# Seven sums over the partitions: two fp32r products of a split operand in place of one fp32 product

## The chip, the cores and the metric

The kernel runs on one core of a Trainium2 chip. The metric is device time in microseconds (us) of one execution, start to end. Before the change it is 1109.1 us, the median of three runs (1109.07 to 1109.46).

Five engines work side by side, each through its own list of instructions in order: TensorE (PE, matmuls), VectorE (DVE), ScalarE (ACT), GpSimd (POOL) and SyncE (SP), which here only issues DMAs. An instruction that has to wait holds up all that stands behind it on its engine. `fp32r` is a 4-byte type that the kernel feeds to PE's fast matmuls; a plain `float32` (fp32) operand makes PE take a slower kind of matmul.

## The reference

One layer of an encoder block over 272 positions (16 learned meta tokens and 256 tokens) of width 2048, all in float32:

```python
hn = rmsnorm(h, mix_norm_g)                # x * rsqrt(mean(x*x) + eps) * g
q_a, k_a, v_a, cq, ckv, k_pe = split(hn @ w_in)
# group A: 8 heads of 2-D neighbourhood attention; q_a and k_a get an rmsnorm per head
# group B: 8 heads of latent attention:
#   q = rmsnorm(rmsnorm(cq) @ w_q_up),  kv = rmsnorm(ckv) @ w_kv_up
#   k = rmsnorm([k_nope, k_pe]),  then a rotation of the last 64 dimensions of q and k
mix = concat(rmsnorm(out_a), rmsnorm(out_b))
h = h + mix @ w_out
h = h + (silu(conv3(rmsnorm(h) @ w_gate)) * (rmsnorm(h) @ w_up)) @ w_down
```

Every rmsnorm needs a sum of squares over the features.

## The kernel before

**Layout and tiling.** Activations stand transposed: features over the 128 partitions, positions along the row (272 columns, or 258 where only the tokens and two meta tokens next to them are needed). A sum over features is therefore a sum over the partitions. The kernel first adds the squares of all 128-row tiles element by element, and then multiplies the one tile that is left with a 128x128 matrix of ones on PE: each output row is the sum over the partitions. That matmul is `ones_sum(sq, n)` (line 763). Both operands of it are fp32.

**Splits.** All large products are made exact enough by splitting: a value is the sum of a high part `hi`, rounded to fp32r, and a low part `lo`, the rest. ACT writes the high part, DVE the low part (`split_plain`, line 976; for the weights `split_hi` and `split_lo`, lines 549 and 567, which write the tiles `whi` and `wlo`). A product is three fp32r matmuls: hi*hi, hi*lo, lo*hi (`mm3`, line 603, recorded as L606, L607, L608). PE's other matmuls are recorded as L278 (`MM`) and its transposes as L284 (`TR`).

**The seven sums.** `ones_sum` is called for: x (`scale_x`, line 795, 272 columns), the query latent (`scale_cq`, 838, 258), the key/value latent (`compressed_kv`, 850, 272), the rotary key (`rotary_key`, 901, 272), the output of each attention group (`group_scale`, 1484, called twice, 258) and h ahead of the MLP (`scale_h`, 1528, 258). The sum of x's squares is added up in the tile `sqx` by POOL, 15 additions in `sum_x` (line 739), each as soon as ACT has squared a tile. When the last is done, the event `ev_sum_x` is set, and `scale_x` goes on: it copies `ones` on DVE into the fp32r tile `ones_r` (for other sums, in `keys` and `small_sums`, that use two fp32r products already), then asks for `ones_sum(sqx, L)`, and makes the norm's factor from its result.

**The norms' weights.** `make_gains` (line 926) multiplies columns of the weight table `vecs` into a tile `gains`: three DVE operations on 128x1, issued when `vecs` has landed. `gains` is used by the keys and queries of the attention heads, from 66 us on.

**What sets the order.** The kernel is written as Python generators, one thread per piece of work. Each `yield` asks for an engine with a cost in ns, or for an event, or for a buffer. A planner (`Flow`, line 99 on) runs them in simulated time when the program is built, and the order in which it serves them is the order of the instructions on each engine. A request can start at the thread's time plus a latency: 700 ns towards PE (`TO_PE`), 200 away from PE, 140 between the others; of several that could start at the same moment, the one with the smaller priority number goes first. The costs are formulas: a `tensor_tensor` of DVE counts 68 + 1.04 ns for each column, so a weight split of 512 columns 600; an fp32 product of 272 columns 460, an fp32r one 124. What the chip does later changes nothing in the order. Buffers come from pools (`Slots`), such as `sps`, two PSUM banks for sums and scores, and `scr`, nine scratch tiles.

Of the kernel before, what the change touches and what calls it, by code (L numbers as in the profile page):

```python
# [10 lines left out]
F32R = mybir.dt.float32r  # L11
# [4 lines left out]
P = 128  # L16
# [4 lines left out]
L = SEQ + N_META  # L21
# [184 lines left out]
def encoder_block(ctx: ExitStack, tc: tile.TileContext, io):  # L206
    nc = tc.nc
    ctx.enter_context(tc.manual_schedule())
    fl = Flow()
# [6 lines left out]
    apool = actx.enter_context(tc.tile_pool(name="apool", bufs=1))  # L216

    def tiles(pool, n, shape, name, dt=F32):
        return [pool.tile(shape, dt, tag=f"{name}{i}", name=f"{name}{i}") for i in range(n)]


    def size(ap):
        n = 1
        for s in ap.shape[1:]:
            n *= s
        return n
# [4 lines left out]
    def columns(*scalars):  # L231
        return sum(not (s is None or isinstance(s, float)) for s in scalars)

    def ACT(out, in_, f, **kw):
        ns = (51 if in_psum(in_) else 93) + 0.833 * size(in_)
        ns += 93 * (columns(kw.get("scale")) + columns(kw.get("bias")) > 0)
        yield "act", ns + 113 * ("accum_out" in kw)
        nc.scalar.activation(out, in_, f, **kw)  # L238

    def TT(out, a, b, op):  # L240
        yield "dve", 68 + 1.04 * size(out)
        nc.vector.tensor_tensor(out, a, b, op)  # L242

    def TS(out, a, s0, s1, *ops):
        yield "dve", 68 + 62 * columns(s0, s1) + (1.04 if in_psum(a) else 0.52) * size(out)
        nc.vector.tensor_scalar(out, a, s0, s1, *ops)  # L246

    def STT(out, a, s, b, op0, op1):
        yield "dve", 68 + 62 * columns(s) + 1.04 * size(out)
        nc.vector.scalar_tensor_tensor(out, a, s, b, op0, op1)  # L250

    def COPY(out, a):
        yield "dve", 68 + 1.04 * size(out)
        nc.vector.tensor_copy(out, a)
# [13 lines left out]
    def cost(l, r):  # L268
        n, m = size(r), l.shape[-1]
        if r.dtype != F32R:  # L270
            return max(1.69 * n, 3.33 * m, 50)
        return 0.445 * n + 3 if n >= 256 else max(0.84 * n, 0.84 * m, 27)

    def MM(items):

        yield "pe", sum(cost(l, r) for _, l, r, _, _ in items)
        for o, l, r, start, stop in items:
            nc.tensor.matmul(o, l, r, start=start, stop=stop)  # L278
# [18 lines left out]
    def one(slots):  # L297
        (t,) = yield slots, 1
        return t
# [172 lines left out]
    n = len(others) - BEHIND  # L472
# [145 lines left out]
    def vec(name, i=0):  # L618
        c = VECS[name] + i
        return vecs[:, c : c + 1]  # L620

    def const(name, n=P):
        return consts[:, CONSTS[name] : CONSTS[name] + n]

    ones = const("ones")
# [126 lines left out]
    ev_sum_x = Event()  # L752


    def rstd(out, v, a):

        yield from ACT(out, v, AF.Ln)
        yield from ACT(out, out, AF.Exp, scale=-0.5)
        yield from ACT(a, out, AF.Square)
        yield from STT(a, v, -0.5, a, ALU.mult, ALU.mult)  # L760
        yield from STT(out, a, 1.5, out, ALU.add, ALU.mult)

    def ones_sum(sq, n):
        s = yield from one(sps)
        yield from MM([(s[:, :n], ones, sq, True, True)])
        return s

    def token_columns(row, small, main):


        yield "pool", 150
        nc.gpsimd.tensor_copy(few_t, repeated(row[:, SEQ:NT], 2))
        pt = yield from one(tps)
        yield from TR(
            [(pt[:4, :P], few_t.rearrange("p c t -> p (c t)")), (pt[:, P : 2 * P], row[:, :P]),
             (pt[:, 2 * P : 3 * P], row[:, P:SEQ])]
        )
        yield from COPY(small, pt[:4, 0:1])
        for c in range(2):
            for i in range(2):  # L780
                j = 2 * c + i
                yield from COPY(main[:, j : j + 1], pt[:, (i + 1) * P : (i + 1) * P + 1])
        fl.put(tps, pt)

    s1 = apool.tile([P, L], F32, name="s1")
    ones_r = apool.tile([P, P], F32R, name="ones_r")
# [5 lines left out]
    ev_em1, ev_s1, ev_em1c, ev_emc, ev_ones = Event(), Event(), Event(), Event(), Event()  # L792
    ev_kr, ev_ekpe = Event(), Event()

    def scale_x():
        yield ev_sum_x
        yield ev_consts
        yield from COPY(ones_r, ones)
        fl.set(ev_ones)
        m1, a = yield scr, 2  # L800
        ss = yield from ones_sum(sqx, L)
        yield from TS(m1[:, :L], ss[:, :L], 1.0 / D_MODEL, EPS, ALU.mult, ALU.add)
        fl.put(sps, ss)
        yield from TS(em1, m1[:, :L], EPS, None, ALU.mult)
        fl.set(ev_em1)
        yield from rstd(s1, m1[:, :L], a[:, :L])
        fl.put(scr, m1)
        fl.put(scr, a)
        fl.set(ev_s1)
        yield from token_columns(em1[:, :NT], em1_s, em1_c)  # L810
        fl.set(ev_em1c)
# [26 lines left out]
    def scale_cq():  # L838
        yield ev_cqs
        yield ev_em1  # L840
        t = sum_cq[:, :NT]
        ss = yield from ones_sum(t, NT)
        yield from STT(t, ss[:, :NT], 1.0 / Q_RANK, em1[:, :NT], ALU.mult, ALU.add)
        fl.put(sps, ss)
        yield from TS(t, t, EPS, None, ALU.mult)
        yield from token_columns(t, emc_s, emc_c)
        fl.put(scr, sum_cq)
        fl.set(ev_emc)

    def compressed_kv(pss):  # L850
        t0, t1, a, b, r = yield scr, 5
        ts = (t0, t1)
        for i, ps in enumerate(pss):
            yield from ACT((a, b)[i][:, :L], ps[:, :L], AF.Square)
        fl.spawn(latent_gained(pss, ts))
        yield from TT(a[:, :L], a[:, :L], b[:, :L], ALU.add)
        yield ev_em1
        ss = yield from ones_sum(a[:, :L], L)
        v = b[:, :L]
        yield from STT(v, ss[:, :L], 1.0 / KV_RANK, em1, ALU.mult, ALU.add)  # L860
        fl.put(sps, ss)
        yield from rstd(r[:, :L], v, a[:, :L])
        for i, t in enumerate(ts):
            fl.spawn(latent_scaled(i, t, r))
        for i in range(2):
            yield ev_ckvs[i]
        for t in (a, b, r):
            fl.put(scr, t)
        fl.set(ev_ckv)
# [55 lines left out]

    def make_gains():
        yield ev_vecs
        yield from STT(gains[:, 0:1], vec("g_naq"), HD ** -0.5, vec("g_nak"), ALU.mult, ALU.mult)
        yield from STT(gains[:, 1:2], vec("g_qn"), QK_DIM ** -0.5, vec("g_kn"), ALU.mult, ALU.mult)
        yield from TS(gains[:, 2:3], vec("g_qp"), QK_DIM ** -0.5, None, ALU.mult)  # L930
        fl.set(ev_gains)
# [44 lines left out]
    def split_plain(hi, lo, src):  # L976
        yield from ACT(hi, src, AF.Copy)
        yield from TT(lo, src, hi.bitcast(F32), ALU.subtract)
# [1048 lines left out]

    fl.spawn(first_loads())
    fl.spawn(make_gains())

    fl.spawn(split_x(), 2)
    fl.spawn(split_hi(), lambda: -1 if 16 < n_split[0] < at[0] + 2 else 2)
    fl.spawn(split_lo(), lambda: -1 if 16 < n_split[1] < at[0] + 2 else 2)
    fl.spawn(square_x(), lambda: 3 if sq_n[0] < 10 else 0)
    fl.spawn(sum_x(), 3)
    fl.spawn(scale_x())
    fl.spawn(scale_cq())
    fl.spawn(attention_weights(), 1)
# [159 lines left out]
```

## Time and profile before

| | |
|---|---|
| median of three runs | 1109.1 us |
| the profiled execution | 1109.03 us, of which the span from first to last instruction is 1107.2 us |
| PE busy | 1101.4 us (99%) |
| DVE busy | 990.3 us (89%) |
| ACT busy | 733.8 us (66%) |
| POOL busy | 140.7 us (13%) |
| granted TensorE clock | 1.0 |
| starts of the seven sums' products on PE | 36.3, 39.4, 45.4, 63.2, 280.0, 296.6 and 388.5 us |
| POOL's additions into `sqx` | 15, from 15.0 us on, the last begins at 34.7 us |
| `gains` on DVE | three operations, 23.2 to 25.7 us |

In the timeline, a row has the start, the time that the instruction (or a run of equal ones) took, the engine, the line, the operation, the output and input tiles, shapes, and how many there are; in brackets stands idle time of the engine before it, and what ended that. Matmuls overlap: a new one can start before the one ahead has ended, so their price is the distance between starts. An fp32 product shows as two matmul rows.

### The profile page before, as it was taken

The numbers are of one execution on the slowest core, as the hardware profiler recorded it, in microseconds if no ns is written. First come the engines' busy times: TensorE is split into PE (matmuls) and PEld (weight loads), VectorE is DVE, ScalarE is ACT, GpSimd is POOL, SyncE is SP. The second block draws the span as 40 slices with busy tenths as digits, with TensorE's granted clock in tenths as the row PEclk, the third lists the DMA queues.
The fourth block names the chain that finished last, engine by engine and source line by source line (L and its number), as shares of the span: only waits on it lengthen the run. The fifth ranks groups of instructions, "written<-read, shape, count | busy, mean of one in ns | idle before, by whom it ended". The sixth has DMA issues, their size and how long they took to land.

```text
span 1107.2 us, 22547 instructions
## 1 busy us (share of the span) xinstructions
PE 1101.4 (99%) x8414; PEld 1062.7 (96%) x8414; DVE 990.3 (89%) x1834; ACT 733.8 (66%) x1467; POOL 140.7 (13%) x202
## 2 busy tenths in 40 slices
PE   9999999999999999999999999999999999999998
PEld 9999999999999999999999999999999988888888
DVE  8879888888868989999999999988988999999984
ACT  8688979898647766656666565655556565655663
POOL 3311222121333400000000000000000011100114
PEclk9999999999999999999999999999999999999999
DMA  9553434444655696657656577777678787777862
GB/s 326 196 171 124 150 125 151 139 162 134 230 188 159 208 342 226 194 189 241 222 196 230 178 244 242 235 236 244 202 277 297 263 297 250 252 258 262 284 250 77
DMA packets 72374, 239.41 MB, mean 216 GB/s; under 512 B 8136, under 2 KB 12744, under 8 KB 72264
## 3 DMA queue, kind: packets, MB, share of 16 engines
q1 hardware_dynamic: 71976, 237.69, 63.7%
q8 instruction: 66, 1.08, 0.4%
q14 instruction: 44, 0.36, 0.1%
q10 hardware_dynamic: 288, 0.27, 0.1%
HBM read 219.44 MB, written 17.83 MB: 214 GB/s over the span
## 4 chain that ended last, share of the span: by engine, by line
PE 93%; ACT 3%; DVE 3%; issue 1%; POOL 0%; DVEq 0%; POOLq 0%; ACTq 0%
PE bank L278 24%; PE bank L606 19%; PE bank L607 19%; PE bank L608 19%; PE bank L1857 6%; PE bank L1858 3%; PE bank L284 2%; ACT whi L238 1%; DVE scr L250 1%; ACT scr L238 1%; DVE wlo L242 0%; PE bank L698 0%; DVE cols L258 0%; ACT mqr L238 0%; DVE p L246 0%
## 5 line engine op out<-in xcount | busy, mean ns | idle before, releaser
L238 ACT ACTIVATE whi<-raw 128x512 fp32r<-128x512 f32 (+2 forms) x479 | 357.8, 764 | 171.8 <-PE bank L607 91.0
L242 DVE TENSOR_TENSOR wlo<-raw,whi 128x512 fp32r<-128x512 f32 (+2 forms) x479 | 415.1, 885 | 46.8 <-ACT whi L238 44.7
L606 PE MATMUL bank<-hl,whi 128*128 128x258 f32 (+2 forms) x1528 | 438.9, 287 | 0.1
L607 PE MATMUL bank<-hl,whi 128*128 128x258 f32 (+2 forms) x1528 | 433.7, 284 | 0.0
L608 PE MATMUL bank<-hl,wlo 128*128 128x258 f32 (+2 forms) x1528 | 432.9, 283 | 0.0
L608 PEld LDWEIGHTS bank<-hl,wlo 128*128 128x128 f32 x1528 | 290.1, 190 | 0.6 <-DVE wlo L242 0.6
L607 PEld LDWEIGHTS bank<-hl,whi 128*128 128x128 f32 x1528 | 289.6, 190 | 0.1
L606 PEld LDWEIGHTS bank<-hl,whi 128*128 128x128 f32 x1528 | 288.5, 189 | 0.5 <-ACT scr L238 0.4
L238 ACT ACTIVATE whi<-quarters 128x1024 fp32r<-128x1024 f32 x88 | 81.5, 950 | 64.7 <-PE bank L1857 44.4
L278 PE MATMUL bank<-whi,act 128*128 128x256 f32 (+1 forms) x420 | 111.5, 317 | 0.0
L1857 PE MATMUL bank<-act,whi 128*128 128x512 f32 x308 | 109.9, 397 | 0.0
L242 DVE TENSOR_TENSOR wlo<-quarters,whi 128x1024 fp32r<-128x1024 f32 x88 | 99.5, 1156 | 10.6 <-ACT whi L238 10.1
L266 POOL TENSOR_TENSOR mt<-mt,mt 128x256 f32<-128x256 f32 x7 | 6.9, 986 | 652.3 <-ACT mt L238 652.3
L1858 PE MATMUL bank<-act,wlo 128*128 128x256 f32 x308 | 86.4, 280 | 0.0
L278 PE MATMUL bank<-whi,sin 128*128 128x512 f32 (+1 forms) x272 | 83.5, 355 | 0.0
L278 PEld LDWEIGHTS bank<-whi,act 128*128 128x128 f32 x420 | 74.1, 189 | 5.7
L1857 PEld LDWEIGHTS bank<-act,whi 128*128 128x128 f32 x308 | 57.8, 188 | 13.8
L278 PE MATMUL bank<-whi,hl 128*128 128x256 f32 x288 | 66.5, 280 | 0.0
L278 PE MATMUL bank<-wlo,act 128*128 128x256 f32 (+1 forms) x210 | 66.3, 315 | 0.0
L238 ACT ACTIVATE whi<-more_raw 128x1024 fp32r<-128x1024 f32 (+2 forms) x46 | 44.1, 962 | 23.9 <-PE bank L607 11.6
L1858 PEld LDWEIGHTS bank<-act,wlo 128*128 128x128 f32 x308 | 58.1, 189 | 1.6
L278 PEld LDWEIGHTS bank<-whi,sin 128*128 128x128 f32 x272 | 49.5, 188 | 7.7
(276 smaller groups left out, 1948.8 us busy)
## 6 DMA issues: line engine op xcount, KB each, us to landing
raw<-in_w_gate SPq DMA_DIRECT2D x83, 512.0 KB, 5.0
raw<-in_w_in SPq DMA_DIRECT2D x52, 512.0 KB, 4.1
raw<-in_w_up_s SPq DMA_DIRECT2D x44, 512.0 KB, 4.8
quarters<-in_w_down_s SPq DMA_DIRECT2D x44, 512.0 KB, 6.9
raw<-in_w_up SPq DMA_DIRECT2D x34, 512.0 KB, 5.4
raw<-in_w_out SPq DMA_DIRECT2D x32, 512.0 KB, 3.9
raw<-in_w_down SPq DMA_DIRECT2D x32, 512.0 KB, 5.0
s_down<-sums SPq DMA_DIRECT2D x22, 512.0 KB, 4.0
```

Of the source, the lines that this page charges most:

```text
L238: nc.scalar.activation(out, in_, f, **kw)
L242: nc.vector.tensor_tensor(out, a, b, op)
L250: nc.vector.scalar_tensor_tensor(out, a, s, b, op0, op1)
L266: nc.gpsimd.tensor_tensor(out, a, b, op)
L278: nc.tensor.matmul(o, l, r, start=start, stop=stop)
L284: nc.tensor.transpose(o, i, ident[:n, :n])
L606: nc.tensor.matmul(ps, whi, xhi, start=start, stop=False)
L607: nc.tensor.matmul(ps, whi, xlo, start=False, stop=False)
L608: nc.tensor.matmul(ps, wlo, xhi, start=False, stop=stop)
L1857: nc.tensor.matmul(ps, whi, x, start=start, stop=False)
L1858: nc.tensor.matmul(ps[:, :n], wlo, x[:, 0, :], start=False, stop=stop)
```

## The change

`ones_sum` now splits its operand first: a new pair of fp32r tiles (`parts_sq`, one pair for all seven calls) takes the high part from ACT and the low part from DVE, and PE multiplies each with `ones_r`, adding both in one PSUM bank. Because `ones_r` has to be there, `ones_sum` waits for the event that its copy sets, and `scale_x` makes that copy before it waits for the sum of x's squares, not after. `make_gains` waits for the sum of x's squares too.

```diff
+    parts_sq = Slots(tiles(apool, 1, [P, 2, L], "parts_sq", F32R))
+
     def ones_sum(sq, n):
+
+        parts = yield from one(parts_sq)
+        hi, lo = (parts[:, i, :n] for i in range(2))
+        yield from split_plain(hi, lo, sq)
+        yield ev_ones
         s = yield from one(sps)
-        yield from MM([(s[:, :n], ones, sq, True, True)])
+        yield from MM([(s[:, :n], ones_r, hi, True, False), (s[:, :n], ones_r, lo, False, True)])
+        fl.put(parts_sq, parts)
         return s
...
     def scale_x():
-        yield ev_sum_x
         yield ev_consts
         yield from COPY(ones_r, ones)
         fl.set(ev_ones)
+        yield ev_sum_x
         m1, a = yield scr, 2
         ss = yield from ones_sum(sqx, L)
...
     def make_gains():
         yield ev_vecs
+        yield ev_sum_x
         yield from STT(gains[:, 0:1], vec("g_naq"), HD ** -0.5, vec("g_nak"), ALU.mult, ALU.mult)
```

## The prediction

> **What bounds the kernel now.** The page comes first: busy times, the chain that ended last, and what an engine waited for.
>
> ```profile
> PE 1101.4 (99%) x8414; PEld 1062.7 (96%) x8414; DVE 990.3 (89%) x1834; ACT 733.8 (66%) x1467; POOL 140.7 (13%) x202
> ...
> PE 93%; ACT 3%; DVE 3%; issue 1%; POOL 0%; DVEq 0%; POOLq 0%; ACTq 0%
> ```
>
> TensorE is the bound from end to end: 93% of the chain is PE. So an edit is worth what it takes from PE's stream of matmuls, or what it makes that stream wait. The seven sums lie in three places; the view of stages shows how full the others are there.
>
> ```profile
> 22.00:36.00 14.00, 13.97 (x111) 13.61 (x110) 13.86 (x23) 13.72 (x34) 10.38 (x10) 1.00 0.67 216
> 36.00:50.00 14.00, 14.00 (x111) 13.64 (x110) 11.44 (x34) 7.88 (x19) 0.88 (x2) 1.00 0.68 228
> 50.00:100.00 50.00, 49.48 (x398) 48.13 (x397) 41.55 (x105) 40.85 (x122) 7.16 (x16) 1.00 0.46 143
> ...
> 200.00:300.00 100.00, 100.00 (x829) 99.06 (x828) 87.36 (x222) 81.64 (x244) 24.59 (x42) 1.00 0.50 164
> ...
> 383.00:430.00 47.00, 47.00 (x394) 46.94 (x393) 40.57 (x83) 32.24 (x58) 2.55 (x2) 1.00 0.80 286
> ```
>
> Columns: stretch, length, then busy time of PE, its weight loads, DVE, ACT, POOL. From 22 to 36 us, right before the first sum, DVE is busy 13.86 of 14.00 us. In the other stretches shown it has an eighth or more to spare. The clock is 1.00 throughout, so it plays no part.
>
> **Part 1: the product itself.** PE's timeline around the first sum (fp32, 272 columns), the fifth (fp32, 258) and a sum that is two fp32r products already:
>
> ```profile
> 36.14 0.29 PE L608 MATMUL bank<-hl,wlo 128*128 128x272 f32 x1
> 36.27 0.62 PE L278 MATMUL bank<-sqx,consts 128*128 128x272 f32 x2
> 36.52 0.49 PE L606 MATMUL bank<-hl,whi 128*128 128x272 f32 x1
> 36.85 0.29 PE L607 MATMUL bank<-hl,whi 128*128 128x272 f32 x1
> ...
> 76.79 0.41 PE L278 MATMUL bank<-late,ones_r 128*128 128x272 f32 x2
> 77.04 0.29 PE L606 MATMUL bank<-hl,whi 128*128 128x272 f32 x1
> ...
> 280.04 0.60 PE L278 MATMUL bank<-sum_b,consts 128*128 128x258 f32 x2
> 280.28 0.47 PE L606 MATMUL bank<-ob,whi 128*128 128x258 f32 x1
> 280.59 0.29 PE L607 MATMUL bank<-ob,whi 128*128 128x258 f32 x1
> 280.71 0.28 PE L608 MATMUL bank<-ob,wlo 128*128 128x258 f32 x1
> ```
>
> Matmuls overlap, so their price is the distance of starts. The first sum and the matmul behind it take 36.85 - 36.27 = 0.58 us; such a matmul alone takes 0.13 (36.14 to 36.27), so the fp32 product costs 0.45. The matmul behind it is where half of that sits: it starts 0.33 before its successor, not 0.13. The two fp32r products cost 77.04 - 76.79 = 0.25, with no mark left on the next matmul. Gain: 0.20. With 258 columns it is (280.59 - 280.04) - 0.12 = 0.43 against 2 x 0.12 = 0.24, gain 0.19. Three sums have 272 columns (x, the kv latent, the rotary key), four have 258 (the q latent, two groups, h): 3 x 0.20 + 4 x 0.19 = **-1.36 us**, and all of it lies on PE. The Trainium skill ("FP8 and Floating Point Precision", TensorE Precision Notes) counts true fp32 as four passes; here it is two recorded matmuls of together 0.45 us, not four of 0.125, so by the page the seven would give 7 x 0.25 = 1.75 and the total below would be 0.4 lower; I go by the rows.
>
> **Part 2: the norms' weights (`make_gains`) move.** Three tiny DVE operations run at 23 to 26 us, and PE shows this:
>
> ```profile
> 22.91 1.02 POOL L746 TENSOR_TENSOR sqx<-sqx,pt 128x272 f32<-128x272 f32 x1 [0.58 <-DMA raw<-in_w_in]
> 23.21 0.73 DVE L250 SCALAR_TENSOR_TENSOR gains<-vecs 128x1 f32<-128x1 f32 x1
> 23.87 0.68 DVE L242 TENSOR_TENSOR wlo<-raw,whi 128x512 fp32r<-128x512 f32 x1
> 24.37 0.29 PE L607 MATMUL bank<-hl,whi 128*128 128x258 f32 x1
> 24.47 0.73 DVE L250 SCALAR_TENSOR_TENSOR gains<-vecs 128x1 f32<-128x1 f32 x1
> 24.60 0.39 PE L608 MATMUL bank<-hl,wlo 128*128 128x258 f32 x1
> 24.82 0.29 PE L606 MATMUL bank<-hl,whi 128*128 128x258 f32 x1
> 25.12 0.49 DVE L250 SCALAR_TENSOR_TENSOR hl<-pt,hl 128x272 fp32r<-128x272 f32 x1
> 25.53 0.14 DVE L246 TENSOR_SCALAR gains<-vecs 128x1 f32<-128x1 f32 x1
> 25.60 0.68 DVE L242 TENSOR_TENSOR wlo<-raw,whi 128x512 fp32r<-128x512 f32 x1
> 26.02 0.28 PE L607 MATMUL bank<-hl,whi 128*128 128x258 f32 x1
> 26.33 0.39 PE L608 MATMUL bank<-hl,wlo 128*128 128x258 f32 x1
> 26.55 0.28 PE L606 MATMUL bank<-hl,whi 128*128 128x258 f32 x1
> ```
>
> They hold DVE for (23.87 - 23.21) + (25.12 - 24.47) + (25.60 - 25.53) = 1.38 us, each ahead of a low part (`wlo`) that PE needs next. PE loses (24.82 - 24.37) - 0.24 = 0.21 and (26.55 - 26.02) - 0.24 = 0.29. With the three gone the low parts come 0.66 and 1.38 earlier, more than the waits. **-0.50 us**, kept if nothing else is late next (part 3).
>
> Behind the sum each would cost between 0.07 (the last one's distance) and 0.73; I take 0.25 for the three, by the last one, since POOL has nothing to do then (it ends its adds at 35.56, see below). The Trainium skill ("SBUF", Who interferes with whom) says that a DVE operation with two SBUF inputs and a GpSimd one that reads SBUF exclude each other; the row agrees (0.73 us for 128x1 beside the add from 22.91 on). If 0.73 held wherever they stand, the wait of part 3 would grow by 1.2 us.
>
> **Part 3: the split ahead of the product.** Each sum now needs ACT (high part), then DVE (low part), then PE. Alone these are small: an ACT pass over 128x272 from this trace is 0.43 us, a DVE one 0.43 (rows below). What counts is the order. The planner sets each engine's order by its own costs. It puts a product at least 700 ns behind the planned end of what feeds it (`TO_PE`), and counts a DVE split of 128x512 as 600. Before, the first sum's thread copies `ones_r` on DVE and only then asks for its product. The chip shows:
>
> ```profile
> 27.09 8.47 POOL L746 TENSOR_TENSOR sqx<-sqx,pt 128x272 f32<-128x272 f32 x7 [1.91 <-ACT pt L238]
> ...
> 28.78 1.18 ACT L238 ACTIVATE late<-bank,vecs 128x258 fp32r<-128x258 f32 x3
> 29.62 1.79 DVE L250 SCALAR_TENSOR_TENSOR late<-bank,vecs,late 128x258 fp32r<-128x258 f32 x4
> ...
> 34.84 2.47 DVE L242 TENSOR_TENSOR wlo<-raw,whi 128x512 fp32r<-128x512 f32 x3
> 37.24 0.21 DVE L254 CAST ones_r<-consts 128x128 fp32r<-128x128 f32 x1
> 37.38 0.68 DVE L242 TENSOR_TENSOR whi<-raw,whi 128x512 fp32r<-128x512 f32 x1
> 37.98 0.68 DVE L242 TENSOR_TENSOR wlo<-raw,wlo 128x512 fp32r<-128x512 f32 x1
> ...
> 44.29 0.43 DVE L242 TENSOR_TENSOR scr<-scr,scr 128x272 f32<-128x272 f32 x1
> 45.65 0.15 DVE L254 COPY emc_s<-bank 4x1 f32<-4x1 f32 x1 [0.93 <-PE bank L284]
> ...
> 39.64 0.43 ACT L238 ACTIVATE s<-scr 128x272 f32<-128x272 f32 x1 [3.74 <-DVE scr L246]
> ```
>
> The copy ran at 37.24 to 37.45, but the product planned 0.7 behind it had started at 36.27. So DVE is 37.45 + 0.70 - 36.27 = 1.9 us late against PE here: beside POOL's adds of x's squares three splits take 37.24 - 34.84 = 2.40, not 1.8, and the work before them is stretched likewise. Today nobody feels it, because the product reads `sqx`, ready at 35.56. After the change the product reads a DVE result, and PE, in order, stands before it. The wait is 1.9 - 0.7 = 1.2, less the rounding up to the next free place between groups of three matmuls (0 to 0.37, mean 0.2), plus the 0.50 that PE has gained in part 2. DVE does not keep its own gain of 1.38: its four operations from 29.62 on take their input from ACT's (28.78 on), whose order and length are unchanged. That is 1.5. Counted forward it is the same: 37.24 for DVE, the three moved operations 0.25, one split 0.60, the low part 0.43, so 38.5; PE's place is three groups later, 36.27 + 9 x 0.126 - 0.50 = 36.9; wait 1.6. I take **+1.5 us**, bounds 0 (the planner finds the low part a place ahead of splits that are not ready) and 2.7 (the 0.73 of part 2).
>
> On ACT the high part stands before the adds' end at 35.56 and holds the weight splits behind it for about a microsecond; ACT then idles 3.74 us before 39.64 anyway, which covers it. Without that cover it would be another 1.3 (0.9 of waiting, 0.4 of work).
>
> At the other six sums I take 0. At the q latent and the kv latent PE is itself 1.5 later than planned, so DVE is late by 0.4 against it, under the 0.7; by 45.65 DVE even idles 0.93. The rotary key, the groups and h have DVE an eighth free, and the results have time: the groups' sums are needed after the first output products, h's after a whole pair of gate tiles. Cover gone, each costs up to 0.43 + 0.43. The early copy of `ones_r` waits for `consts`, long landed where the planner puts it: 0.
>
> **Sum**, against the profiled execution's 1109.03 (span 1107.2 and 1.8 around it; the median is 1109.1): -1.36 - 0.50 + 1.50 = -0.36, so 1108.7.
>
> **Rivals.**
> - *No wait at the first sum.* Only gains are left: -1.86, 1107.2. For it: the planner might put the product later. Against: DVE's 1.9 us are measured, and the lead it leaves is 0.7.
> - *The planner's new order clears old waits.* Everything behind 22 us is sorted anew. From 50 to 100 us PE issues 398 matmuls; at the rate of 200 to 300 us (829 in 100) it would be 414, so some 16 x 0.12 = 2 us may be waits there. All gone: 1108.7 - 2.0 = 1106.7. Against: nothing in the change aims at them, and an order can lose as much.
> - *Slower: DVE's lateness is not used up by the first wait.* If the gains, three low parts and the splits that ACT held back keep DVE over 0.7 us late at the q and kv latents too, PE waits 1.5 at each of three sums: -1.86 + 4.5 = +2.6, 1111.7. It decides from a DVE lateness of 0.7 on at 39 us. For it: DVE is nearly full until 44.7. Against: the idle 0.93 before 45.65.
> - *The product's saving isn't PE's.* If the gap behind an fp32 product were there anyway, part 1 gives half: 1109.4. The row at 77.04 speaks against.
>
> **How the numbers follow.** Forecast 0.48, no wait 0.20, new order 0.15, slower 0.12, half the saving 0.05. What a measurement can tell from no change is about 0.2%, 2.2 us: under 1106.9 or over 1111.3. Faster: the new order, and a third of "no wait" with luck in the order, 0.22. Slower 0.12; the rest 0.66. The range runs from 1106.8 to 1110.7: below it lies half of the new order, above it the slower case; its upper part holds the 2.7 bound (1109.9) and some loss by order.
>
> **What would show it.** Two fp32r matmuls per sum, 0.25 apart from the next, seven times. No gap in PE at 24.6 and 26.3. One new gap of 1.2 to 1.7 us in PE before the first sum's product, put down to DVE's low part, with that part at about 38. Wrong if PE has no such gap, if it has gaps at the second and third sum, or if waits between 50 and 300 us move the end by more than this sum.

## The result, and the profile after

The changed kernel takes 1112.07 us (median, 1111.67 to 1113.54); the kernel before, in the same session, 1109.18 (1108.95 to 1109.84). The ratio is 1.0026, 95% interval 1.0017 to 1.0036: slower by 2.9 us, where 0.4 less was forecast. The profiled execution took 1112.18 us.

The page of the changed kernel: span, busy times, and the chain that ended last.

```profile
span 1110.1 us, 22546 instructions
PE 1100.5 (99%) x8414; PEld 1062.4 (96%) x8414; DVE 994.0 (90%) x1841; ACT 737.0 (66%) x1474; POOL 143.4 (13%) x202
PE 93%; ACT 2%; DVE 2%; issue 1%; DMA 1%; POOL 0%; SPq 0%; DVEq 0%; POOLq 0%; ACTq 0%
```

PE is the bound as before, with 0.9 us less to do (1101.4 before); DVE and ACT have seven instructions more each, the splits. The span is 2.9 us longer all the same, so PE must stand idle longer. Where, the view of stages tells. Of the kernel before, the stretch from 48 to 131 us (columns as in the prediction: stretch, length, busy PE, weight loads, DVE, ACT, POOL, clock, DMA share, GB/s):

```profile
48.00:131.00 83.00, 82.31 (x675) 80.78 (x674) 70.75 (x182) 71.28 (x220) 14.57 (x33) 1.00 0.46 147
```

Of the changed kernel, the stages of the prediction and that stretch:

```profile
22.00:36.00 14.00, 13.87 (x111) 13.54 (x110) 13.86 (x22) 11.85 (x31) 8.89 (x10) 1.00 0.66 223
36.00:50.00 14.00, 12.91 (x104) 12.56 (x103) 11.96 (x36) 9.46 (x22) 1.44 (x2) 1.00 0.69 222
...
200.00:300.00 100.00, 100.00 (x831) 99.03 (x831) 87.41 (x229) 82.42 (x249) 23.99 (x43) 1.00 0.48 162
383.00:430.00 47.00, 47.00 (x395) 46.97 (x394) 41.66 (x82) 34.12 (x61) 4.46 (x4) 1.00 0.83 295
...
48.00:131.00 83.00, 79.96 (x658) 78.44 (x657) 70.39 (x182) 70.48 (x217) 18.60 (x33) 1.00 0.44 149
```

In the two stages shown behind 200 us nothing is lost. From 36 to 50 us PE is busy 12.91 of 14.00 instead of 14.00: the wait at the first sum, which the prediction has. From 48 to 131 us it is busy 79.96 instead of 82.31, so 2.35 us are lost where the prediction had none. The waits of PE, of the kernel before (for what, on what; us in total, times, longest):

```profile
PE bank L698 <- DVE em L695: 1.1, 1, 1.1
PE bank L278 <- POOL sq8r L266: 0.5, 2, 0.3
```

and of the changed kernel:

```profile
PE bank L278 <- POOL sq8r L266: 2.0, 2, 1.7
PE bank L278 <- DVE gains L246: 1.1, 1, 1.1
PE bank L698 <- DVE em L695: 1.1, 1, 1.1
PE bank L606 <- ACT qraw L238: 0.7, 2, 0.4
PE bank L278 <- DVE mkp L242: 0.5, 1, 0.5
PE bank L284 <- POOL p L266: 0.2, 1, 0.2
```

The second line is the first sum (the profile names the DVE operation right behind the low part). The others that are new or longer (`sq8r`, `qraw`, `mkp`, `p`) have no part in the seven sums: they belong to the heads' queries, keys and scores.

**PE's lag** puts it in order. Take the start of the n-th matmul of PE's commonest kind (L606, the first of each triple; 1860 in both kernels) and subtract that of the kernel before. Worked out from the two traces:

| from, to (us, time of before) | lag grows by | what lies there | forecast |
|---|---|---|---|
| to 19.8 | +0.30 | start, landing of the first DMAs | |
| 19.8 to 32.1 | -0.34 | the norms' weights are gone from here | -0.50 |
| 32.1 to 37.1 | +0.39 - 0.45 | a new wait at 35.2; the first product has not run yet (it had before) | 0 |
| 37.1 to 38.6 | +1.72 | first sum: two products and their wait; with the -0.45 above +1.27 | -0.20 + 1.50 |
| 38.6 to 60 | -0.41 | q and kv latent | -0.39 |
| 60 to 64.4 | -0.20 | rotary key | -0.20 |
| 64.4 to 131.4 | **+2.21** | heads of both groups | 0 |
| 131.4 to 266.8 | +0.01 | | 0 |
| 266.8 to 310 | -0.33 | the two groups' sums | -0.38 |
| 310 to 416 | -0.15 | h's sum | -0.19 |
| 416 to the end | +0.21 | | 0 |

Together +2.96. One line of this table is out of the forecast by more than 0.5 us, and it is 2.21. The first line differs from execution to execution (-0.28 to +1.25 at 19.8 us in the traces of the kernels below). Where work is in another order, a lag inside such a stretch can be off by a few tenths of a microsecond and more; the marks from 38.6 us on stand where the lag over all 8414 matmuls is the same.

The places that the prediction named, in the changed kernel's PE timeline:

```profile
24.59 0.29 PE L607 MATMUL bank<-hl,whi 128*128 128x258 f32 x1
24.75 0.39 PE L608 MATMUL bank<-hl,wlo 128*128 128x258 f32 x1
24.97 0.28 PE L606 MATMUL bank<-hl,whi 128*128 128x258 f32 x1
...
35.22 0.29 PE L607 MATMUL bank<-hl,whi 128*128 128x272 f32 x1
35.63 0.39 PE L608 MATMUL bank<-hl,wlo 128*128 128x272 f32 x1
35.86 0.29 PE L606 MATMUL bank<-hl,whi 128*128 128x272 f32 x1
...
37.39 0.39 PE L278 MATMUL bank<-parts_sq,ones_r 128*128 128x272 f32 x1
38.87 0.39 PE L278 MATMUL bank<-parts_sq,ones_r 128*128 128x272 f32 x1 [1.08 <-DVE gains L246]
39.10 0.29 PE L606 MATMUL bank<-hl,whi 128*128 128x272 f32 x1
...
286.51 0.41 PE L278 MATMUL bank<-parts_sq,ones_r 128*128 128x258 f32 x2
286.75 0.49 PE L284 MATMUL bank<-ident,p 128*128 128x128 f32 x3
```

The high part's product starts at 37.39; the low part's could follow 0.13 later, at 37.52, and starts at 38.87: a wait of 1.35. The fifth sum takes 286.75 - 286.51 = 0.24. The gap at 24.6 has shrunk to (24.97 - 24.59) - 0.24 = 0.14, the one at 26.3 to 0.09, and there is one of (35.86 - 35.22) - 0.25 = 0.39 at 35.2.

DVE of the changed kernel in front of the first sum:

```profile
26.57 4.61 DVE L242 TENSOR_TENSOR wlo<-raw,whi 128x512 fp32r<-128x512 f32 x5
...
37.64 0.15 DVE L250 SCALAR_TENSOR_TENSOR gains<-vecs 128x1 f32<-128x1 f32 x1
37.71 0.68 DVE L242 TENSOR_TENSOR whi<-raw,whi 128x512 fp32r<-128x512 f32 x1
38.31 0.15 DVE L250 SCALAR_TENSOR_TENSOR gains<-vecs 128x1 f32<-128x1 f32 x1
38.38 0.43 DVE L242 TENSOR_TENSOR parts_sq<-sqx,parts_sq 128x272 fp32r<-128x272 f32 x1
```

The low part ends at 38.81 (forecast 38.5). The norms' weights cost 0.15 each now, not 0.73, as taken.

### The profile page after: what moved, and what is told of

It is laid out like the page before. It is cut to its first block, busy times and chain, and to the rows that moved or that the text cites. A ratio compares the mean times of both kernels' runs of the same rounds, so it can differ in the third digit from the quotient of the medians.

```text
span 1110.1 us, 22546 instructions
## 1 busy us (share of the span) xinstructions
PE 1100.5 (99%) x8414; PEld 1062.4 (96%) x8414; DVE 994.0 (90%) x1841; ACT 737.0 (66%) x1474; POOL 143.4 (13%) x202
## 4 chain that ended last, share of the span: by engine, by line
PE 93%; ACT 2%; DVE 2%; issue 1%; DMA 1%; POOL 0%; SPq 0%; DVEq 0%; POOLq 0%; ACTq 0%
PE bank L278 25%; PE bank L606 19%; PE bank L607 19%; PE bank L608 19%; PE bank L1866 6%; PE bank L1867 3%; PE bank L284 2%; ACT whi L238 1%; DVE wlo L242 1%; ACT scr L238 1%; DMA scr<-scr 0%; DMA raw<-in_w_in 0%; DVE scr L250 0%; PE bank L698 0%; POOL sq8r L266 0%
## 5 line engine op out<-in xcount | busy, mean ns | idle before, releaser
L606 PE MATMUL bank<-hl,whi 128*128 128x258 f32 (+2 forms) x1528 | 437.8, 287 | 0.0
L606 PEld LDWEIGHTS bank<-hl,whi 128*128 128x128 f32 x1528 | 288.7, 189 | 0.1
L238 ACT ACTIVATE whi<-more_raw 128x1024 fp32r<-128x1024 f32 (+2 forms) x46 | 44.1, 962 | 24.6 <-PE bank L607 9.8
```

What stands on the lines that cost most here:

```text
L606: nc.tensor.matmul(ps, whi, xhi, start=start, stop=False)
```

## The experiments

Theory at the start: the splits are more work on DVE and ACT, and the waits from 62 us on are theirs. Its rival: the planner, told of other costs, issues the same work in another order from 48 us on (in the traces, PE's order is another up to about 200 us), and it is that order which PE waits in. Growth of the lag is that from 60 to 131 us, and from there to 266 us. It holds the rotary key's product, so 0.2 less where that one is two fp32r products; 131 us lies inside the stretch of another order in some kernels, so the sum of the two columns is surer than each.

| kernel | us | ratio (95%) | 60 to 131 | 131 to 266 |
|---|---|---|---|---|
| the change | 1112.07 | 1.0026 (1.0017 to 1.0036) | +2.01 | +0.01 |
| `gains_only` | 1108.95 | 1.0000 (0.9991 to 1.0008) | +0.01 | -0.07 |
| `sums_only` | 1111.82 | 1.0025 (1.0016 to 1.0034) | +1.91 | +0.07 |
| `x_fp32` | 1111.59 | 1.0021 (1.0012 to 1.0030) | +1.91 | 0.00 |
| `late3` | 1108.78 | 0.9996 (0.9987 to 1.0005) | -0.03 | +0.01 |
| `late3_gains` | 1109.12 | 0.9997 (0.9989 to 1.0006) | -0.03 | +0.09 |
| `after_order_fp32` | 1113.42 | 1.0033 (1.0020 to 1.0046) | +2.19 | +0.05 |
| `before_order_split` | 1112.37 | 1.0026 (1.0016 to 1.0037) | +0.02 | +0.16 |
| `sq8r_dve` | 1112.02 | 1.0024 (1.0014 to 1.0033) | +1.93 | +0.19 |
| `rotlate300` | 1109.23 | 0.9999 (0.9990 to 1.0008) | -0.70 | +0.40 |
| `only_rot` | 1110.15 | 1.0007 (0.9998 to 1.0016) | -0.30 | +0.64 |
| `only_ckv` | 1114.45 | 1.0044 (1.0030 to 1.0058) | +0.87 | +3.01 |
| `after_two_slipped` | 1110.09 | 1.0010 (1.0001 to 1.0019) | -0.09 | +0.31 |
| `slip_ckv` | 1110.15 | 1.0008 (0.9999 to 1.0017) | -0.36 | +0.59 |
| `slip_rot` | 1114.13 | 1.0043 (1.0030 to 1.0057) | +0.61 | +2.95 |
| `five_slipped` | 1108.92 | 0.9996 (0.9987 to 1.0005) | 0.00 | +0.19 |

### One part of the change alone

`gains_only` is the kernel before with the one line of `make_gains`; `sums_only` is the change without it.

```diff
     def make_gains():
         yield ev_vecs
+        yield ev_sum_x
```

> Only the norms' weights move behind the sum of x's squares; the seven sums stay fp32. If the two waits of PE at 24.6 and 26.3 us come from the three DVE operations, they vanish and nothing else moves: about 0.5 us under before, 1108.7. If those waits have another cause, or come back a few us later, the time stays at 1109.2. If the move itself is what made the changed kernel slower, this is slower than before: above 1110.

> Only the seven sums change; the norms' weights stay where they were. If the loss comes with the split sums (the wait at the first, and new waits between 60 and 130 us), this is as slow as the changed kernel or up to 0.5 us slower: 1112 to 1112.6. If the moved weights are the cause, it is at or under before: 1107.8 to 1109.2.

Measured: the move alone does nothing, the sums alone do all of it. Why the move gives nothing is to be seen on DVE of `gains_only`:

```profile
24.89 1.02 DVE L250 SCALAR_TENSOR_TENSOR hl<-pt,hl 128x272 fp32r<-128x272 f32 x1
...
26.85 5.19 DVE L242 TENSOR_TENSOR wlo<-raw,whi 128x512 fp32r<-128x512 f32 x5
...
37.64 0.15 DVE L250 SCALAR_TENSOR_TENSOR gains<-vecs 128x1 f32<-128x1 f32 x1
```

The 0.73 of a weight operation was not its own work but waiting beside POOL's additions. With the operations gone, what stands behind them on DVE waits in their place: `hl` takes 1.02 (0.49 before, at 25.12), and the five low parts 5.19. In the kernel before they were:

```profile
26.61 3.09 DVE L242 TENSOR_TENSOR wlo<-raw,whi 128x512 fp32r<-128x512 f32 x5
```

Beside them POOL's last seven additions take 6.86 us in `gains_only`, 8.47 before: here it is DVE that waits more and POOL less. What PE gains by 32 us (0.11) it gives back at 35.6 (0.14), where it stands before a low part.

`x_fp32` is the change with x's sum left in fp32:

```diff
-        ss = yield from ones_sum(sqx, L)
+        ss = yield from one(sps)
+        yield from MM([(ss[:, :L], ones, sqx, True, True)])
```

> As changed, but the sum of x's squares alone is one fp32 product as before, so PE has nothing to wait for there. If the 1.35 us before the second half of the first sum are lost for good, the time falls by that less 0.2: about 1110.9, the waits at 60 to 130 us staying. If they were made good later, it stays at 1112. As the order behind 36 us is sorted anew once more, a time outside 1109 to 1112.5 would show that the order weighs more than the wait.

Measured: 0.5 us less than the change. The wait of 1.35 is gone, but not all of it; PE of `x_fp32` stands at the q latent's product instead:

```profile
40.18 0.28 PE L278 MATMUL bank<-parts_sq,ones_r 128*128 128x258 f32 x1
40.99 0.39 PE L278 MATMUL bank<-parts_sq,ones_r 128*128 128x258 f32 x1 [0.53 <-DVE parts_sq L242]
```

(40.99 - 40.18) - 0.12 = 0.69. So DVE's lateness at this point is real, and the first product that reads DVE meets it: the prediction's mechanism. The loss behind 60 us is nearly untouched (+1.91), so that wait is not its cause.

`late3` is the kernel before, with the change in the last three sums alone (two groups, h); `late3_gains` has the move of the norms' weights and of `ones_r`'s copy as well.

```diff
-        ss = yield from ones_sum(sums, NT)
+        ss = yield from ones_sum2(sums, NT)     # the change's ones_sum
...
-        ss = yield from ones_sum(sum_h, NT)
+        ss = yield from ones_sum2(sum_h, NT)
```

> Only the sums of the two attention groups and of h become two fp32r products; up to 272 us every engine has the order of before. If each product saves 0.19 us on PE and its split is covered, the time is 0.57 under before: 1108.6, and PE's progress up to 272 us is that of before. If the saving is eaten by waits for the splits (0.4 to 0.9 each), it is 1109.5 to 1111. If fp32r saves nothing on PE, 1109.2.

> The moved weights and the early copy of the ones as changed, and two fp32r products for the sums of the two groups and of h only; up to 272 us the planner serves all requests in the order of before. If the two gains add up (0.23 measured for the weights, 0.40 for the three late sums), 1108.5, under both kernels. If the weights' gain is lost again, 1108.8; if the early part of the change makes the waits at 60 to 130 us without its sums, 1110 or more.

Measured: no difference that the runs can tell. In the traces PE's lag falls by 0.71 in `late3` (+0.30 at 276 us, -0.41 at 416) and by 0.63 in `late3_gains`, against 0.57 forecast: the saving is there, and up to 416 us nothing beside it is lost. (The traced execution of `late3`, 1110.36 us, is the slowest of its eleven; it loses 1.5 us between 500 and 560 us, where the edit changes nothing.)

### The order or the work

`after_order_fp32` asks the planner for every step of the change, so that all comes in the change's order, but issues no split and one fp32 product. `before_order_split` is the opposite: the splits are issued, and the planner isn't told, so the order is that of before (`make_gains` stays too).

```diff
 # after_order_fp32, against the change
-        yield from split_plain(hi, lo, sq)
+        yield "act", 93 + 0.833 * n
+        yield "dve", 68 + 1.04 * n
         yield ev_ones
         s = yield from one(sps)
-        yield from MM([(s[:, :n], ones_r, hi, True, False), (s[:, :n], ones_r, lo, False, True)])
+        yield "pe", 2 * cost(ones_r, hi)
+        nc.tensor.matmul(s[:, :n], ones, sq, start=True, stop=True)
```

```diff
 # before_order_split, against the kernel before
         s = yield from one(sps)
-        yield from MM([(s[:, :n], ones, sq, True, True)])
+        nc.scalar.activation(hi, sq, AF.Copy)
+        nc.vector.tensor_tensor(lo, sq, hi.bitcast(F32), ALU.subtract)
+        yield "pe", cost(ones, sq)
+        nc.tensor.matmul(s[:, :n], ones_r, hi, start=True, stop=False)
+        nc.tensor.matmul(s[:, :n], ones_r, lo, start=False, stop=True)
```

> The changed kernel's order on every engine (the planner gets the same requests and costs), but the seven sums are single fp32 products of the squares, and the split's ACT and DVE instructions are not issued; the result is the same. If the loss comes from the new order, it stays: the first wait goes (-1.35), the products cost 1.36 more, the waits at 60 to 130 us remain, about 1112. If it comes from the split's own work and its waits, it is gone: 1108.7, before less the moved weights.

> The order of before on every engine, with the split's two instructions slipped in where each sum's thread asks for its product, and two fp32r products in place of the fp32 one; the planner does not know of the split. The norms' weights stay. If the order makes the waits at 60 to 130 us, there are none beyond those of before, and the time is before less 1.36 plus a wait at the sums whose split has no lead (1.6 at the first, up to 1 at the q latent and the two groups): 1109 to 1111. If the split's work makes the waits at 60 to 130 us, they are here too, and it is 1111 or more.

The first is 4.1 us slower than before by the median, the second 3.1, and the totals alone would settle nothing. (Four of the first one's five runs had a granted clock of 0.998 and took 1112.97 to 1113.56; the traced one, at 1.0, took 1111.58, and its lag at the end is 2.42.) The stretch does. Stages of `after_order_fp32`:

```profile
48.00:131.00 83.00, 79.99 (x657) 78.40 (x656) 70.17 (x180) 70.90 (x219) 18.68 (x33) 1.00 0.45 146
```

and what its PE waited for:

```profile
PE bank L278 <- POOL sq8r L266: 2.1, 2, 1.7
...
PE bank L606 <- ACT qraw L238: 0.6, 2, 0.4
PE bank L278 <- DVE mkp L242: 0.5, 1, 0.5
```

Without a single split PE loses the same 2.3 us (79.99 against 82.31) at the same places. In `before_order_split`, with all seven splits, the lag grows by 0.02 from 60 to 131 us and by 0.16 from there to 266. Its loss lies elsewhere, in PE's waits:

```profile
PE bank L771 <- DVE ones_r L254: 1.1, 1, 1.1
...
PE bank L284 <- DVE s L250: 0.5, 1, 0.5
```

These are the first sum again, and a transposition at 398 us; another 0.7 is lost at 282 us, where the group's product stands behind a split for which nobody left time. So the theory of the work fell: behind the rotary key's sum it is the order.

`after_two_slipped` then tests the account as a whole. It is the change, except that the planner isn't told of the kv latent's and the rotary key's splits; the order from 48 to 270 us is then that of before.

```diff
-        ss = yield from ones_sum(a[:, :L], L)
+        ss = yield from ones_sum_slipped(a[:, :L], L)     # kv latent
...
-        ss = yield from ones_sum(t[:, :L], L)
+        ss = yield from ones_sum_slipped(t[:, :L], L)     # rotary key
```

(`ones_sum_slipped` issues the split without a request, as in `before_order_split`, and asks for the product at its fp32 cost.)

> The changed kernel, all seven sums as two fp32r products and the gains moved, but for the kv latent's and the rotary key's sums the planner is not told of the splits (they are issued behind the squares all the same, and the product is asked for at its fp32 cost), so that the stretch from 48 to 125 us keeps the order of before. Theory (the new order of 62 to 97 us costs 2.1 us of the 2.9): about 1110.0, PE's lag behind before flat from 62 to 97 us, the wait of 1.35 at the first sum still there. Rival (the splits' own work in that stretch costs it): about 1112, with the lag growing by some 2 us there. If the two sums' products wait for their splits because nobody left them a lead, up to 0.5 each on top of 1110.

Measured 1110.09, as the theory of the order had it: 2.0 us less than the change with the same work on every engine. Its stages show it too, where PE is busy 82.14 us against 79.96 in the change:

```profile
48.00:131.00 83.00, 82.14 (x675) 80.67 (x674) 70.16 (x187) 71.53 (x219) 15.11 (x33) 1.00 0.46 149
```

### What in the order costs the time

The longest of the new waits, 1.7 us at 76 us, has a mechanism of its own. POOL of the kernel before:

```profile
74.75 0.33 POOL L266 TENSOR_TENSOR sq8r<-sq,sq8r 128x8 fp32r<-128x8 f32 x1 [0.17 <-DVE sq8r L254]
```

POOL of the changed kernel:

```profile
75.98 1.83 POOL L266 TENSOR_TENSOR sq8r<-sq,sq8r 128x8 fp32r<-128x8 f32 x1 [0.17 <-DVE sq8r L254]
```

DVE of the changed kernel at that time:

```profile
75.75 0.68 DVE L242 TENSOR_TENSOR wlo<-raw,whi 128x512 fp32r<-128x512 f32 x1
76.35 0.43 DVE L242 TENSOR_TENSOR late<-scr,late 128x272 fp32r<-128x272 f32 x1
76.70 0.68 DVE L242 TENSOR_TENSOR wlo<-raw,whi 128x512 fp32r<-128x512 f32 x1
77.31 0.43 DVE L242 TENSOR_TENSOR scr<-kr,scr 128x272 f32<-128x272 f32 x1
77.66 0.17 DVE L250 SCALAR_TENSOR_TENSOR v<-cols,emc_c 128x4 f32<-128x4 f32 x1
```

The same 8 columns take 1.83 us instead of 0.33, and end at 77.81, when a run of four two-input operations on DVE is over. The Trainium skill ("SBUF — State Buffer", Who interferes with whom) has a DVE operation with two SBUF inputs and a GpSimd one that reads SBUF exclude each other; the rows agree. `sq8r_dve` moves that operation to DVE and keeps the change's order:

```diff
-        yield from PTT(
+        yield "pool", 90 + 2.7 * 4 * n
+        nc.vector.tensor_tensor(
             r[:, 1, : 4 * n], f[:, : 4 * n], r[:, 0, : 4 * n].bitcast(F32), ALU.subtract
         )
```

> The changed kernel's order, but the low part of the few queries' squares (128x4 or 128x8, eight times) is issued on DVE at the same place of the program instead of on POOL. If PE's 1.8 us wait at 76 us is POOL being kept from its operands by DVE's operations with two inputs in SBUF, it vanishes, and the time falls by 1.3 to 1.8: 1110.3 to 1110.8. If the operation is late because of what it waits for, DVE stands in its place, the wait stays, and the time is 1112 or more.

Measured 1112.02, no gain. PE's waits in `sq8r_dve`:

```profile
PE bank L278 <- DVE sq8r L1081: 0.8, 2, 0.5
PE bank L284 <- POOL p L266: 0.7, 1, 0.7
```

PE's wait at 76 us has gone from 1.67 to 0.34, and at 84 us its lag is 1.17 where the change has 2.51. But at 96.7 us it is 2.91, as in the change (2.92): PE has lost there what it had won. `sums_only` and `x_fp32`, whose order is that of the change but for a few places, say the same: POOL's operation takes 0.51 us in `sums_only`, the lag of the two does not rise from 72 to 84 us, and by 131 us they too have lost 1.91. So POOL's long operation is one place at which the loss shows, not its cause. DVE is busy 9.94 of 10.00 us from 87 to 97 us in `sq8r_dve` as in the change and in the kernel before; that it is DVE which sets the pace there is likely by this, but not shown.

Which request changes the order? `only_rot` and `only_ckv` are the change with one of the two sums as fp32r products and the other six in fp32; `rotlate300` is the kernel before, with no instruction changed, where the planner is told that the rotary key's squares are ready 0.3 us later.

```diff
 # only_rot: all calls but the rotary key's; only_ckv: all but the kv latent's
-        ss = yield from ones_sum(...)
+        ss = yield from ones_sum0(...)       # one fp32 product, as before
```

```diff
 # rotlate300, in rotary_key of the kernel before
+        fl.cur.t += 300.0
         ss = yield from ones_sum(t[:, :L], L)
```

> As changed, but of the seven sums only the rotary key's (at 63 us) is two fp32r products. This alone makes the planner sort 48 to 125 us anew, into an order that is neither that of before nor that of the changed kernel. If the order of before is a good one and others lose, PE falls 1 to 2.3 us behind before between 62 and 97 us: 1110 to 1111.2. If only the changed kernel's own order is bad, or the split's work as such was the cause (one split is a seventh of it), 1108.8.

> As changed, but of the seven sums only the key/value latent's (at 45 us) is two fp32r products. It sorts 48 to 125 us anew too, into a third order. If the order of before is a good one and others lose: 1110 to 1111.2, the loss between 62 and 97 us. If only the changed kernel's own order is bad: 1108.8.

> The kernel of before with every instruction as it was; only the planner is told that the rotary key's squares are there 0.3 us later than it thinks, which sorts 48 to 125 us anew, into a fourth order. If the order alone decides, the time moves by up to 2 us with no work changed, most likely slower, 1110 to 1111.2, with PE level with before up to 60 us. If the order does not matter, 1109.2 as before.

`only_ckv` is slower than the whole change, 1114.45, with one of its seven splits; `only_rot` can't be told from before (its trace is 1.25 us behind at 19.8 us already). `rotlate300` has another order again and costs nothing: a new order is not a loss by itself.

Last, the full change with one of the two splits planned and the other slipped in, and a version put together from the harmless parts: `slip_ckv` slips the kv latent's and plans the rotary key's, `slip_rot` the other way; `five_slipped` leaves x's and the q latent's sums in fp32 and the norms' weights where they were, slips both, and has the last three as in the change.

> The changed kernel, where only the kv latent's split is issued without the planner knowing, and the rotary key's is planned as in the change. That gives a third order from 48 to 125 us (neither that of before nor that of the change). Theory 1 (the 2 us of 62 to 97 us belong to the one particular order of the change, and an order is worth what chance makes of it): the lag behind before from 62 to 131 us is something else than the 2.3 of the change, anything from -0.5 to +4; time 1109.6 to 1114. Theory 2 (planning a split in this stretch costs 2 us wherever it stands, about 1 for each of the two sums): the lag grows by about 1, time about 1111.

> The changed kernel, where only the rotary key's split is issued without the planner knowing, and the kv latent's is planned as in the change; a fourth order from 48 to 125 us. Theory 1 (each order has its own price): a lag from 62 to 131 us that is not that of the change, anything from -0.5 to +4. Theory 2 (about 1 us for each planned split in the stretch): about +1, time about 1111.

> A version put together from the runs so far: the sums of x and of the q latent stay fp32, and make_gains and the copy of ones_r stay where they were; the kv latent's and the rotary key's splits are issued without the planner knowing, and the groups' two and h's are as in the change. The order of every engine up to 270 us is that of before. Theory: no wait at the first sum, no loss by order, five products cheaper by 0.2 each, less what the unplanned splits may make them wait: 1109.2 - 1.0 = 1108.2, bounds 1108.0 and 1109.0. Rival (splits cost their work on ACT and DVE even there): 1109.2 or more.

Stages of `slip_ckv`:

```profile
48.00:131.00 83.00, 82.08 (x677) 80.74 (x676) 70.12 (x180) 71.12 (x219) 15.55 (x33) 1.00 0.45 148
131.00:250.00 119.00, 118.61 (x982) 117.13 (x981) 105.27 (x279) 103.55 (x323) 26.48 (x53) 1.00 0.45 145
```

and of `slip_rot`:

```profile
48.00:131.00 83.00, 81.62 (x670) 79.93 (x669) 69.61 (x182) 71.17 (x220) 14.69 (x33) 1.00 0.43 143
131.00:250.00 119.00, 117.67 (x964) 115.03 (x964) 103.75 (x271) 99.94 (x313) 27.17 (x52) 1.00 0.44 143
```

Of the kernel before, the second of these stages is:

```profile
131.00:250.00 119.00, 118.92 (x988) 117.75 (x987) 105.01 (x282) 103.21 (x324) 26.67 (x54) 1.00 0.45 144
```

The two do the same work, and differ by 4.0 us. "About 1 us for each planned split" is out: planning the rotary key's costs nothing (1110.15, like `after_two_slipped` with none planned), planning the kv latent's costs 4, planning both 2. `slip_rot` has nearly the order of `only_ckv` and nearly its growth up to 266 us (+3.56, +3.88); `slip_ckv` that of `only_rot` (+0.23, +0.34): the price goes with the order, whatever else the kernel does. Of five orders, that of before among them, the two with the kv latent's split planned lose 2.0 and 3.6 to 3.9 us; the others lose or gain 0.3 at most. The place is not the same: the change loses its 2 us before 131 us and nothing behind, `slip_rot` and `only_ckv` most of theirs behind (+2.95, +3.01; from 131 to 250 us PE of `slip_rot` issues 964 matmuls, before 988). In the traces PE's order is another than that of before up to about 272 us in these two, and up to about 143 us in `only_rot`, `slip_ckv` and `rotlate300`.

`five_slipped` came to 1108.92, inside its bounds (1108.0 to 1109.0) but 0.7 above the value taken. In its trace the lag falls by 0.70 over the last three sums; the two slipped ones give nothing: the kv latent's because its low part's product now starts 0.4 us behind the high part's, and the rotary key's 0.21 (0.49 at 60 us, 0.28 at 64.2) is lost again by 66 us. Neither it nor `late3` can be told from the kernel before by its time.

**What stays open.** Why an order with the kv latent's split planned costs PE 2 to 4 us, before 131 us in one and behind it in the other, is not settled. In those kernels the kv latent's product stands about 1.3 us later in PE's list (in the change at 47.89 with a lag of 1.2, before at 45.38), so its norm's factor comes later, but no experiment moved that product alone.

## Why the prediction was wrong

**Part 1 was right.** Forecast -1.36. The pair of products and the step to the next matmul cost 0.24 to 0.25 at four sums, 0.33 at the rotary key's and h's; the lag falls by 0.41 at the two latents (forecast 0.39), 0.20 at the rotary key (0.20), 0.33 at the groups (0.38) and 0.15 at h (0.19). The rival by which half of the saving isn't PE's fell.

**Part 2 was wrong, by 0.5.** The step "With the three gone the low parts come 0.66 and 1.38 earlier" took the 0.73 for time that goes with the operation. It was time in which DVE waited beside POOL, and what stands behind inherits it (`hl` 0.49 to 1.02). PE did gain 0.34 by 32 us, and gave back 0.39 at 35.2; `gains_only` measures 1.0000.

**Part 3 was right at the first sum, in part by luck.** Forecast: one new gap of 1.2 to 1.7 us at the first sum's product, behind DVE's low part at about 38. Measured: 1.35, the low part at 38.38 to 38.81, and +1.47 on the lag with the product's own saving taken out (1.27 + 0.20). It stands between the two products, not before the first: the high part was there in time. Two parts of the estimate were off and made up for each other: PE had kept nothing of part 2's 0.50 by then, which makes the wait shorter, and the product stands six matmuls (two groups) further back in PE's list, not three groups, which makes it longer by 0.38. As forecast, ACT's idle time covered the high part, and no gap followed at the second and third sum. The slower rival, three sums waiting 1.5 each, is therefore out, though its 1111.7 lies close to the result.

**The step that failed is "At the other six sums I take 0"**, and with it the case of a new order. The splits there are indeed hardly a burden: `after_two_slipped` has them all, and its lag grows by 0.22 from 60 to 266 us. What costs is that the planner was told of them. The prediction had seen this ("Everything behind 22 us is sorted anew"), and sized it (2 us), but only as a gain; that an order can lose as much stood there as an argument against the gain, with no case, price or chance of its own. It lost 2.2 (64 to 131 us). Of the three things that would make the prediction wrong, the last came true: waits between 50 and 300 us moved the end by more than its sum.

Sum with the measured terms: -1.29 for the products (x's by the forecast), +0.05 for the norms' weights, +1.47 at the first sum, +2.22 by order, is +2.45. With the +0.30 of the start and the +0.21 behind 416 us, about which the forecast says nothing, that is the 2.96 between the two traces; the medians differ by 2.9.

## What to carry to other kernels

Where one planner orders all engines from costs, an edit has two prices: the work it adds, and the new order of all that is planned behind it; no sign of the second was found in the profile of before, and here it could be larger than everything else (-0.3 to +3.9 us by 266 us). Give it a case on both sides in a forecast, and test it by issuing the new work in the old order, and the old work in the new order. And an operation that is long only because another engine keeps it waiting may save nothing when it is moved: here, both times, the time was lost again behind it.

## What the runs showed of the hardware

- A POOL operation on 8 columns took 1.83 us behind four two-input DVE operations in a row, 0.33 in another order; a DVE operation on one column 0.73 beside POOL's additions, 0.15 after them. With the three operations of the norms' weights taken away, the wait passed on to what stood behind them (`hl` 0.49 to 1.02).
- A high and a low product of one sum can stand apart for 1.35 us, and the second then takes 0.39 instead of 0.29 in its row, with the next matmul 0.23 behind it instead of 0.13: about 0.1 for PE to go on after a wait.
